# A ring of six places, four front transfers onto all partitions, and gathers that run upwards

## The chip, the cores and the metric

The kernel runs on one NeuronCore of a Trainium2 chip. Its engines are TensorE (PE), VectorE (DVE), ScalarE (ACT), GpSimd (POOL) and SyncE (SP); each runs its own instruction stream, and they meet through semaphores. Transfers between memory and the on-chip SBUF are carried by 16 DMA engines, which the queues of SP, ACT and POOL share. The metric is the device time of one execution in microseconds (us); the number that counts is the median over several runs.

## The reference

Eight batches of 8192 rows of 512 numbers are masked by a length, summed cumulatively along the rows, and the sum at half the length is taken; that one row per batch is multiplied by a 512x512 matrix.

```python
B, S, D = 8, 8192, 512                       # x: B x S x D float32
pos = np.arange(S)[None, :, None]
mask = (pos < lengths[:, None, None]).astype(np.float32)
cs = np.cumsum(x * mask, axis=1)
midpoints = (lengths // 2).clip(0)
mid_features = cs[np.arange(B), midpoints, :]
return np.matmul(mid_features[:, None, :], w).squeeze(1)
```

So output row b is the sum of the rows 0 to length//2 of batch b (as far as the mask lets them count), times `w`. Lengths are drawn between 16 and 8191; in the draw that is timed, half a length goes up to 3858 rows. No cumulative sum is needed, only a sum of the first rows of each batch, and which rows those are is known only on the chip.

## The kernel before

The sum is made by TensorE: a matmul whose weights are 0 or 1 adds rows of `x` into one PSUM row per batch (`s_ps`). Four consecutive rows form a group of 8 KB, which lies on one partition, so a chunk is 128 groups (1 MB) and takes four products, one for each row u of the group (`add`, L295). The four products go to four column groups of the array and are summed at the end.

**The front.** The first 256 rows of every batch are loaded blind, before the lengths are known. SP issues eight transfers (L117-L122), one per batch, of 64 groups each: even batches onto partitions 0 to 63 of `xf`, odd ones onto 64 to 127. Batch 7 leaves out its first 128 rows here; they come late, as `xb`, one row per partition (L195). Pairs of batches then form four chunks, for which VectorE makes the weights `wf`.

**The rest.** Rows from 256 on are gathered. VectorE works out from the lengths how many groups each batch needs, numbers them through in one list over all batches, and writes for every chunk c the row numbers `idx[:, c]`; entries past the end get a number out of bounds, and nothing is moved for them. It does this for all 61 chunks that the longest lengths could need (`ge`, `z`, `idx`), then makes weights for all 61 (`early`, `wc`). Each VectorE step waits for the one before it (`step`, L206-L210), and every one of them shows up in the profile with line L210.

GpSimd issues one indirect transfer per chunk (L173) into a ring of eight places `xt`, the chunk c into place c % 8. It and TensorE go downwards, from the count of needed chunks to chunk 0, and each chunk has code of its own. To get into it, both jump through a tree of compares (`enter`, L139-L155) past the chunks that this draw does not need: 25 of 61 are used. Chunk 0 is the one with padding and has a place of its own, `xz`, which ScalarE fills with zeros before. A place is free when TensorE has counted it into `s_free` (L327); GpSimd waits for that at L188. Behind the last gather, on the same queue, GpSimd issues `xb` and two transfers for `w` (L195-L198).

**The end.** When the last chunk and `xb` are in, VectorE copies `s_ps` to SBUF in four quarters, TensorE folds the four column groups and turns the result over (L336, four matmuls into four PSUM tiles), VectorE copies these four, TensorE multiplies by `w` (L344), VectorE copies the result, and SP and ACT each store half of it (L135).

Of the kernel before, what the change touches and what calls it, by code (L numbers as in the profile page):

```python
# [11 lines left out]
P = 128  # L12
# [3 lines left out]
def kernel(  # L16
# [13 lines left out]

# [6 lines left out]
    R = 8  # L37
    UB = S // U
    HEAD = 256
    HU = HEAD // U  # L40
    PAIRS = B // 2
    C = -(-B * (S // 2 // U + 1 - HU) // P)
# [12 lines left out]
    def sem(name):  # L55
        return tc.alloc_semaphore(name)

    xf = sb("xf", [P, PAIRS, U * D])
    xb = sb("xb", [P, D])
    xt = sb("xt", [P, R, U * D])  # L60
    xz = sb("xz", [P, U * D])
# [4 lines left out]
    k_f = sb("k_f", [1, B])  # L66
    qe = sb("qe", [1, B])
    up_i = sb("up_i", [1, 1], I32)
    count = sb("count", [1, 1], I32)
    pad = sb("pad", [1, 1])  # L70
    row = sb("row", [1, 4 * B])
# [4 lines left out]
    base = sb("base", [P, 1], I32)  # L76
    rank4 = sb("rank4", [P, 1])
    rank = sb("rank", [P, 1])
    q_i = sb("q_i", [P, C], I32)
    v_i = sb("v_i", [P, C * U], I32)  # L80
    f_i = sb("f_i", [P, U], I32)
    f_m = sb("f_m", [P, U], I32)
    q = sb("q", [P, C])
    v4 = sb("v4", [P, C * U])
    z = sb("z", [P, C, B + 1])
    ge = sb("ge", [P, C, B])
    idx = sb("idx", [P, C], I32)
    early = sb("early", [P, C, U, B])
    wc = sb("wc", [P, C, U, B])
    wf = sb("wf", [P, PAIRS * (U * B + 2)])  # L90
# [9 lines left out]
    mf_ps = [ps(f"mf_ps{k}", [P, D]) for k in range(KC)]  # L100
    o_ps = ps("o_ps", [P, D])
    bc_ps = ps("bc_ps", [P, D])

    s_full = [sem(f"full{c}") for c in range(C)]
    s_front = [sem(f"front{k}") for k in range(PAIRS)]
    s_back = sem("back")
    s_w = [sem(f"w{k}") for k in range(2)]
    s_len, s_out, s_pool, s_dve, s_pe, s_free, s_zero = (
        sem(n) for n in ("len", "out", "pool", "dve", "pe", "free", "zero"))

    END = "gather_end"
    LAST = slice(D - P, D)
    QUARTERS = [slice(k, D - P, KC - 1) for k in range(KC - 1)] + [LAST]


    def sync(sp):
        for b in range(B):  # L117
            skip = P if b == B - 1 else 0
            at = 64 * (b % 2)
            sp.dma_start(out=xf[at + skip // U:at + HU, b // 2],  # L120
                         in_=x[b, skip:HEAD].rearrange("(q u) d -> q (u d)", u=U),
                         ).then_inc(s_front[b // 2], 16)  # L122
        store(sp, 0)
        sp.wait_ge(s_out, 32)


    def scalar(act):
        act.dma_start(out=lens[:], in_=lens_words).then_inc(s_len, 16)
        act.memzero(xz[:])  # L129
        act.memzero(xf[64:64 + P // U, PAIRS - 1]).then_inc(s_zero, 1)  # L130
        store(act, 2)
# [6 lines left out]

    def enter(eng, name, count):  # L139

        def node(lo, hi, label):
            with nc.body(label, valid_engines=[eng.engine]):
                mid = (lo + hi) // 2
                eng.br_cmp(count, mid, target(mid + 1, hi), target(lo, mid), "IS_GT")
            for a, e in ((mid + 1, hi), (lo, mid)):
                if a < e:
                    node(a, e, target(a, e))

        def target(lo, hi):
            if lo == hi:  # L150
                return f"{name}_c{lo - 1}" if lo else f"{name}_tail"
            return f"{name}_n{lo}_{hi}"

        eng.br(target(0, C))
        node(0, C, target(0, C))  # L155


    def gpsimd(pool):
# [7 lines left out]
        pool.iota(f_i[:], pattern=[[1, U]], base=0, channel_multiplier=U)  # L166
        pool.iota(fold_i[:], pattern=[[-1, B]], base=128, channel_multiplier=1)
        pool.iota(v_i[:], pattern=[[P * U, C], [1, U]], base=HEAD, channel_multiplier=0,  # L168
                  ).then_inc(s_pool, 1)
        pool.sem_inc(s_free, R)  # L170

        def gather(to, c):
            pool.indirect_dma_start(  # L173
                out=to, out_offset=None, in_=xu,
                in_offset=bass.IndirectOffsetOnAxis(ap=idx[:, c:c + 1], axis=0),
                bounds_check=B * UB - 1, oob_is_err=False,
            ).then_inc(s_full[c], 16)
# [4 lines left out]
        pool.wait_ge(s_zero, 1)  # L182
        enter(pool, "gp", n)
        for c in range(C - 1, -1, -1):
            with nc.body(f"gp_c{c}", valid_engines=[pool.engine]):
                pool.wait_ge(s_dve, marks["idx"])
                if c:
                    pool.sem_inc(s_free, -1)._wait_ge(s_free, 1)  # L188
                    gather(xt[:, c % R], c)
                    pool.br(f"gp_c{c - 1}")  # L190
                else:
                    gather(xz[:], c)
                    pool.br("gp_tail")
        with nc.body("gp_tail", valid_engines=[pool.engine]):
            pool.dma_start(out=xb[:], in_=x[B - 1, :P]).then_inc(s_back, 16)  # L195
            pool.dma_start(out=wt[:, :KC - 1],
                           in_=w[:D - P].rearrange("(p k) d -> p k d", k=KC - 1)).then_inc(s_w[0], 16)
            pool.dma_start(out=wt[:, KC - 1], in_=w[LAST]).then_inc(s_w[1], 16)  # L198
            pool.drain()
            pool.br(END)  # L200

# [4 lines left out]
    def vector(dve):  # L206
# [6 lines left out]
        def mark(name):  # L213
# [8 lines left out]
        mark("ones")  # L222
        dve.wait_ge(s_pool, 5)
        step(ts, out=p4[:], in0=p_i[:], scalar1=2, scalar2=None, op0=ALU.logical_shift_right)
        step(stt, out=rank[:], in0=p4[:], scalar=-63.0, in1=base[:], op0=ALU.mult, op1=ALU.add)
        step(ts, out=q[:], in0=q_i[:], scalar1=rank[:], scalar2=None, op0=ALU.add)
        step(ts, out=z[:, :, B], in0=q[:], scalar1=float(FAR), scalar2=None, op0=ALU.add)
        dve.wait_ge(s_len, 16)
        step(ts, out=l8[:], in0=lens[:, ::2], scalar1=3, scalar2=None, op0=ALU.logical_shift_right)
        step(ts, out=k_f[:], in0=l8[:], scalar1=float(1 - HU), scalar2=0.0, op0=ALU.add, op1=ALU.max)  # L230
        step(dve.tensor_tensor_scan, out=qe[:], data0=k_f[:], data1=zero[:, :B], initial=0.0,
             op0=ALU.add, op1=ALU.add)
        step(ts, out=up_i[:], in0=qe[:, B - 1:], scalar1=float(P - 1), scalar2=None, op0=ALU.add)
        step(ts, out=count[:], in0=up_i[:], scalar1=7, scalar2=None, op0=ALU.logical_shift_right)
        mark("count")
        step(stt, out=pad[:], in0=count[:], scalar=float(P), in1=qe[:, B - 1:], op0=ALU.mult,
             op1=ALU.subtract)
        step(stt, out=row[:, :B], in0=qe[:], scalar=pad[:], in1=k_f[:], op0=ALU.add,
             op1=ALU.subtract)
        step(ts, out=row[:, B:B + 1], in0=pad[:], scalar1=-1.0, scalar2=float(HU - FAR),  # L240
             op0=ALU.mult, op1=ALU.add)
        step(ts, out=row[:, B + 1:2 * B], in0=k_f[:, :B - 1], scalar1=-1.0, scalar2=float(UB),
             op0=ALU.mult, op1=ALU.add)
        step(ts, out=l2[:], in0=lens[:, ::2], scalar1=1, scalar2=None, op0=ALU.logical_shift_right)
        step(stt, out=row[:, 2 * B:3 * B], in0=l2[:], scalar=1.0, in1=lens[:, ::2], op0=ALU.add,
             op1=ALU.min)
        step(stt, out=row[:, 3 * B:], in0=row[:, :B], scalar=float(U), in1=row[:, 2 * B:3 * B],
             op0=ALU.mult, op1=ALU.add)
        mark("row")
        dve.wait_ge(s_pe, 1)  # L250
        starts, jumps, rows, ends = (bc_ps[:, k * B:(k + 1) * B] for k in range(4))
        step(tt, out=ge[:], in0=q[:].unsqueeze(2).to_broadcast((P, C, B)),
             in1=starts.unsqueeze(1).to_broadcast((P, C, B)), op=ALU.is_ge)
        step(tt, out=z[:, :, :B], in0=ge[:], in1=jumps.unsqueeze(1).to_broadcast((P, C, B)),
             op=ALU.mult)
        step(dve.tensor_reduce, out=idx[:], in_=z[:], axis=AX.X, op=ALU.add)
        mark("idx")
        step(dve.memset, wf[:], 0.0)
        step(dve.memset, wb[:], 0.0)
        dve.wait_ge(s_pool, 6)  # L260
        step(ts, out=f_m[:], in0=f_i[:], scalar1=HEAD - 1, scalar2=None, op0=ALU.bitwise_and)
        diag = wf[:].rearrange("p (f e) -> p f e", f=PAIRS)
        for h in range(2):
            at = slice(64 * h, 64 * h + 64)
            step(tt, out=diag[at, :, h:h + U * B:B],
                 in0=f_m[at].unsqueeze(1).to_broadcast((64, PAIRS, U)),
                 in1=rows[at, h::2].unsqueeze(2).to_broadcast((64, PAIRS, U)), op=ALU.is_lt)
# [3 lines left out]
        step(tt, out=early[:].rearrange("p c u b -> p (c u) b"),  # L271
             in0=v4[:].unsqueeze(2).to_broadcast((P, C * U, B)),
             in1=ends.unsqueeze(1).to_broadcast((P, C * U, B)), op=ALU.is_lt)
        step(tt, out=wc[:], in0=early[:], in1=ge[:].unsqueeze(2).to_broadcast((P, C, U, B)),
             op=ALU.mult)
        step(ts, out=fold_m[:], in0=fold_i[:], scalar1=31, scalar2=None, op0=ALU.bitwise_and)
        step(tt, out=wb[:, B - 1:], in0=p_i[:], in1=rows[:, B - 1:], op=ALU.is_lt)
        step(dve.memset, fold[:], 0.0)
        step(ts, out=fold[:, :, 0], in0=fold_m[:], scalar1=0, scalar2=None, op0=ALU.is_equal)
        mark("w")  # L280
        dve.wait_ge(s_pe, 2)
# [7 lines left out]
        dve.wait_ge(s_pe, 3 + KC)  # L289
        step(dve.tensor_copy, out=o_sb[:], in_=o_ps[:, :P])  # L290
        mark("out")


    def tensor(pe):
        def add(j, weights, rows, cols=slice(0, D)):  # L295
# [95 lines left out]
```

## Time and profile before

| | us |
|---|---|
| three runs | 95.44, 94.98, 94.63 |
| median | 94.98 |
| the profiled execution | 95.83 |
| its span in the profile | 93.7 |
| PE busy | 48.6 |
| POOL busy | 28.7 |
| DVE busy | 14.2 |
| ACT busy | 5.1 |

The span runs from the first to the last instruction of the program in the profile; the execution's own time is 2.1 us longer. The page cuts the span into 40 slices and gives for each how busy the engines were, the share of the DMA engines' time that was used, and the rate in GB/s. Queue q1 in its third part carries the transfers that SP issues, q0 those of GpSimd; instructions are fetched through q8 and q14. Matmuls of 32-bit numbers appear as two each, and a chunk as eight.

### The profile page before, as it was taken

How to read it: one execution, taken by the hardware profiler on the slowest of the kernel's cores; microseconds unless marked ns; L12 is line 12 of the kernel's file. 1: busy time of each engine (PE TensorE's matmuls, PEld its weight loads, DVE VectorE, ACT ScalarE, POOL GpSimd, SP SyncE). 2: the span in 40 equal slices, each digit the busy share in tenths (PEclk: the TensorE clock that was granted, in tenths of full speed). 3: DMA queues.
4: the chain of work that ended last, by engine and by line, in shares of the span. 5: the costliest groups of instructions: out<-in, count | busy, mean ns of one | idle time of the engine just before them, and what ended most of it. 6: DMA issues, size and time to landing. Idle time of an engine off the chain costs nothing. (4 is left out here: it accounts for less than half of the span.)

```text
span 93.7 us, 856 instructions
## 1 busy us (share of the span) xinstructions
PE 48.6 (52%) x298; PEld 7.4 (8%) x298; DVE 14.2 (15%) x43; ACT 5.1 (5%) x3; POOL 28.7 (31%) x41
## 2 busy tenths in 40 slices
PE   1820834265200029995444477533677887479820
PEld 0120000000000002210000000000000000001700
DVE  3868995000000000000000000000000000000710
ACT  3980000000000000000000000000000000000000
POOL 5300002778710000677748423553830000000000
PEclk9999999999999999999999555999555555966998
DMA  0999999999999999999999999999999999995000
GB/s 0 238 224 224 220 224 213 224 224 399 413 420 430 406 423 413 420 416 430 413 427 416 430 427 413 430 402 427 416 430 416 427 413 430 408 410 227 9 10 4
DMA packets 4557, 31.26 MB, mean 334 GB/s; under 512 B 621, under 2 KB 653, under 8 KB 909
## 3 DMA queue, kind: packets, MB, share of 16 engines
q0 software_dynamic: 3904, 27.21, 70.5%
q1 hardware_dynamic: 626, 3.94, 19.2%
q8 instruction: 5, 0.08, 0.4%
q14 instruction: 2, 0.02, 0.1%
q10 hardware_dynamic: 20, 0.01, 0.0%
HBM read 31.46 MB, written 0.02 MB: 336 GB/s over the span
## 5 line engine op out<-in xcount | busy, mean ns | idle before, releaser
L296 PE MATMUL s_ps<-xt,wc 128*8 128x512 f32 x192 | 33.5, 805 | 27.1 <-DMA xt<-in_x_dram,idx 16.5
L173 POOL DMA_INDIRECT xt<-in_x_dram,idx x24 | 24.0, 1001 | 38.6 <-POOLq L188 34.4
L296 PE MATMUL s_ps<-xf,wf 128*8 128x512 f32 x32 | 7.6, 1040 | 9.9 <-DMA xf<-in_x_dram 6.6
L210 DVE COPY s_sb<-s_ps 128x128 f32<-128x128 f32 x4 | 1.2, 292 | 71.2 <-PE s_ps L296 71.1
L296 PEld LDWEIGHTS s_ps<-xt,wc 128*8 128x8 f32 x192 | 3.7, 93 | 56.9 <-DMA xt<-in_x_dram,idx 39.1
L304 PE MATMUL s_ps<-zero 1*32 1x512 f32 x8 | 1.9, 1055 | 1.9 <-DVE ones L210 1.9
L210 DVE TENSOR_TENSOR wc<-early,ge 128x1952 f32<-128x1952 f32 x1 | 2.2, 2193 | 0.0
L210 DVE TENSOR_TENSOR early<-v,bc_ps 128x1952 f32<-128x1952 f32 x1 | 2.2, 2187 | 0.0
L129 ACT ACTIVATE xz<-xz 128x2048 uint32<-128x2048 uint32 x1 | 1.9, 1909 | 0.0
L130 ACT ACTIVATE xf<-xf 32x2048 uint32<-32x2048 uint32 x1 | 1.9, 1905 | 0.0
L296 PE MATMUL s_ps<-xz,wc 128*8 128x512 f32 x8 | 1.8, 980 | 0.0
L296 PEld LDWEIGHTS s_ps<-xf,wf 128*8 128x8 f32 x32 | 0.5, 90 | 15.4 <-DMA xf<-in_x_dram 11.9
L336 PE MATMUL mf_ps<-fold,s_sb 128*128 128x32 f32 x8 | 1.4, 286 | 0.4 <-DVE s_sb L210 0.4
L307 PE MATMUL bc_ps<-row,ones 1*128 1x32 f32 x2 | 0.6, 408 | 1.6 <-DVE row L210 1.6
L129 ACT ACT_TABLE_LOAD x1 | 1.3, 1283 | 1.5 <-SPq L47 1.5
L344 PE MATMUL o_ps<-wt,mf_sb 128*32 128x128 f32 x32 | 1.3, 285 | 0.0
L336 PEld LDWEIGHTS mf_ps<-fold,s_sb 128*128 128x128 f32 x8 | 1.2, 188 | 0.8 <-DVE s_sb L210 0.7
L173 POOL DMA_INDIRECT xz<-in_x_dram,idx x1 | 1.0, 993 | 0.3 <-issue 0.3
L168 POOL IOTA v_i<- 128x244 int32 x1 | 0.9, 857 | 0.0
L210 DVE COPY mf_sb<-mf_ps 128x32 f32<-128x32 f32 x4 | 0.8, 192 | 0.4
L210 DVE TENSOR_TENSOR ge<-q,bc_ps 128x488 f32<-128x488 f32 x1 | 0.7, 664 | 0.7 <-PE bc_ps L307 0.7
L160 POOL IOTA base<- 32x1 int32 x4 | 0.5, 124 | 0.8 <-SPq L47 0.6
(49 smaller groups left out, 13.2 us busy)
## 6 DMA issues: line engine op xcount, KB each, us to landing
xf<-in_x_dram SPq DMA_DIRECT2D x7, 512.0 KB, 9.3
wt<-in_w_dram POOLq DMA_DIRECT2D x1, 768.0 KB, 19.4
xt<-in_x_dram,idx POOLq DMA_INDIRECT x24, 15.6
xf<-in_x_dram SPq DMA_DIRECT2D x1, 256.0 KB
xb<-in_x_dram POOLq DMA_DIRECT2D x1, 256.0 KB, 18.1
wt<-in_w_dram POOLq DMA_DIRECT2D x1, 256.0 KB, 19.5
lens<-in_lengths_dram ACTq DMA_DIRECT2D x1, 0.1 KB
xz<-in_x_dram,idx POOLq DMA_INDIRECT x1, 18.4
```

Of the source, the lines that this page charges most:

```text
L129: act.memzero(xz[:])
L130: act.memzero(xf[64:64 + P // U, PAIRS - 1]).then_inc(s_zero, 1)
L160: pool.iota(base[32 * k:32 * k + 32], pattern=[[0, 1]], base=64 * (k % 2) + 8 * (k // 2) + 63 * 8 * k, channel_multiplier=16).then_inc(s_p ...
L168: pool.iota(v_i[:], pattern=[[P * U, C], [1, U]], base=HEAD, channel_multiplier=0,).then_inc(s_pool, 1)
L173: pool.indirect_dma_start(out=to, out_offset=None, in_=xu, in_offset=bass.IndirectOffsetOnAxis(ap=idx[:, c:c + 1], axis=0), bounds_check=B ...
L210: do(*args, **kw).then_inc(s_dve, 1)
L296: return pe.matmul(s_ps[32 * j:32 * j + B, cols], lhsT=weights, rhs=rows, start=False, stop=False, skip_group_check=True, tile_position=(0 ...
L304: pe.matmul(to[32 * j:32 * j + 32, :width], lhsT=zero[:, :32], rhs=zero[:, :width], start=True, stop=False, skip_group_check=True, tile_po ...
L307: pe.matmul(bc_ps[:, :4 * B], lhsT=ones[:], rhs=row[:], start=True, stop=True,).then_inc(s_pe, 1)
L336: pe.matmul(mf_ps[k][:, :4 * B], lhsT=s_sb[:, k * P:(k + 1) * P], rhs=fold[:].rearrange("p b r -> p (b r)"), start=True, stop=True).then_i ...
L344: mm = pe.matmul(o_ps[32 * j:32 * j + 32, :P], lhsT=mf_sb[:, k], rhs=wt[:, k, j * P:(j + 1) * P], start=False, stop=(k == KC - 1), skip_gr ...
```

## The change

**The front** is four transfers instead of eight, each of two batches: group q of batch 2f goes to partition 2q of chunk f, that of batch 2f+1 to partition 2q+1. Batch 7's first 256 rows are in it too; its next 128 rows are what comes late as `xb` (`BACK`), and its gathers begin at row 384 (`R0`).

**One ring.** `xt` has six places and holds the front as well: blind chunks in places 0 to 3, gathered chunk c in place (c + 4) % 6. ScalarE clears places 4 and 5 at the start, `xf` and `xz` are gone. A gather waits for TensorE's count of finished chunks, `s_done`.

**TensorE loops.** The blind chunks have their own code; after them six bodies, one for each place, are run round and round, with a compare against the number of chunks, a step down of `s_wr` and a wait for `s_full[s]` against a register. Since a body's weights must lie at a fixed address, they lie in `wr`, six places too; ScalarE copies the weights of each chunk from `wc` into its place, in a loop of its own that waits for `s_done` against a register.

**GpSimd runs upwards**: gather 0 stands in its first block of code, chunks 1, 2, 3 and so on follow behind the tail's code, each with a compare that leaves for the tail (a jump back) once the count is reached. The tail loads `w` in three parts instead of two.

**VectorE** makes the row numbers in two parts, 8 chunks first (gather 0 waits for those alone), then 53; the weights as well. What TensorE broadcasts comes in two rows, `row` and `row2`. Eleven small fills come first. The weights of the blind chunks for even and odd partitions are made by two steps over all partitions.

**Fewer copies**: `s_ps` is copied in two halves instead of four quarters, the folded result as one copy instead of four, and the eight matmuls that clear PSUM become two.

```diff
-    R = 8
+    R = 6
 def sync(sp):
-        for b in range(B):
-            skip = P if b == B - 1 else 0
-            at = 64 * (b % 2)
-            sp.dma_start(out=xf[at + skip // U:at + HU, b // 2],
-                         in_=x[b, skip:HEAD].rearrange("(q u) d -> q (u d)", u=U),
-                         ).then_inc(s_front[b // 2], 16)
+        for f in range(PAIRS):
+            sp.dma_start(out=xt[:, f],
+                         in_=x[2 * f:2 * f + 2, :HEAD].rearrange("b (q u) d -> q b (u d)", u=U),
+                         ).then_inc(s_front[f], 16)
...
 def scalar(act):
-        act.memzero(xz[:])
-        act.memzero(xf[64:64 + P // U, PAIRS - 1]).then_inc(s_zero, 1)
-        store(act, 2)
+        for s in range(PAIRS, R):
+            act.memzero(xt[:, s]).then_inc(s_zero, 1)
+        act.wait_ge(s_dve, marks["w0"])
+        for s in range(PAIRS, R):
+            act.copy(out=weights_of(s), in_=wc[:, s - PAIRS]).then_inc(s_wr, 1)
...
+        for s in range(R):
+            with nc.body(f"ac_0_{s}", valid_engines=[act.engine]):
+                act.br_cmp(left, R + s, f"ac_1_{s}", "ac_end", "IS_GT")
+            with nc.body(f"ac_1_{s}", valid_engines=[act.engine]):
+                act.wait_ge(s_done, free)
+                col = act.snap(free)
+                act.copy(out=weights_of(s),
+                         in_=wc[:, bass.ds(col + (R - PAIRS - 1), 1)].rearrange("p c e -> p (c e)"),
+                         ).then_inc(s_wr, 1)
+                act.reg_add(free, free, 1)
+                if s == R - 1:
+                    act.reg_sub(left, left, R)
+                act.br(f"ac_0_{(s + 1) % R}")
...
 def gpsimd(pool):
+        def gather(c):
+            s = (c + PAIRS) % R
+            if c < R - PAIRS:
+                pool.wait_ge(s_zero, c + 1)
+            else:
+                pool.wait_ge(s_done, c + PAIRS - R + 1)
             pool.indirect_dma_start(
-                out=to, out_offset=None, in_=xu,
+                out=xt[:, s], out_offset=None, in_=xu,
...
-        enter(pool, "gp", n)
-        for c in range(C - 1, -1, -1):
-            with nc.body(f"gp_c{c}", valid_engines=[pool.engine]):
-                pool.wait_ge(s_dve, marks["idx"])
...
+        pool.wait_ge(s_dve, marks["idx0"])
+        gather(0)
+        pool.wait_ge(s_dve, marks["count"])
+        pool.load(n, count[:])
+        pool.wait_ge(s_dve, marks["idx"])
+        pool.br("gp_1")
         with nc.body("gp_tail", valid_engines=[pool.engine]):
...
+        for c in range(1, C):
+            with nc.body(f"gp_{c}", valid_engines=[pool.engine]):
+                pool.br_cmp(n, c, f"gp_go{c}", "gp_tail", "IS_GT")
+            with nc.body(f"gp_go{c}", valid_engines=[pool.engine]):
+                gather(c)
+                pool.br(f"gp_{c + 1}" if c + 1 < C else "gp_tail")
...
 def vector(dve):
+        table(0, C1)
+        mark("idx0")
...
+        table(C1, C)
         mark("idx")
...
-        for k in range(KC):
-            step(dve.tensor_copy, out=s_sb[:, k * P:(k + 1) * P], in_=s_ps[:, QUARTERS[k]])
+        for at in HALVES:
+            step(dve.tensor_copy, out=s_sb[:, at], in_=s_ps[:, at])
         mark("s")
-        for k in range(KC):
-            dve.wait_ge(s_pe, 3 + k)
-            step(dve.tensor_copy, out=mf_sb[:, k], in_=mf_ps[k][:, :4 * B])
+        dve.wait_ge(s_pe, 4)
+        step(dve.tensor_copy, out=mf_sb[:], in_=mf_ps[:])
...
 def tensor(pe):
+        def chunk(s):
+            for u in range(U):
+                mm = add(u, weights_of(s)[:, u * B:(u + 1) * B], xt[:, s, u * D:(u + 1) * D])
+            mm.then_inc(s_done, 1)
+
         pe.wait_ge(s_dve, marks["front"])
         for f in range(PAIRS):
...
+            pe.wait_ge(s_front[f], 16)
+            chunk(f)
+        pe.br(f"pe_0_{PAIRS}")
+        for s in range(R):
+            with nc.body(f"pe_0_{s}", valid_engines=[pe.engine]):
+                pe.br_cmp(left, s, f"pe_1_{s}", "pe_end", "IS_GT")
+            with nc.body(f"pe_1_{s}", valid_engines=[pe.engine]):
+                pe.sem_inc(s_wr, -1)._wait_ge(s_wr, 1)
+                pe.wait_ge(s_full[s], full)
+                chunk(s)
+                if s == R - 1:
+                    pe.reg_sub(left, left, R)
+                if s == PAIRS - 1:
+                    pe.reg_add(full, full, 16)
+                pe.br(f"pe_0_{(s + 1) % R}")
```

More of the change, by code (lines that the diff above doesn't have):

```diff
@@ L65 @@
     l2 = sb("l2", [1, B], I32)
-    k_f = sb("k_f", [1, B])
-    qe = sb("qe", [1, B])
+    kk = sb("kk", [1, B])
+    negk = sb("negk", [1, B])
+    jump = sb("jump", [1, B - 1])
+    r0 = sb("r0", [1, B])
+    mm_ = sb("mm_", [1, B])
+    row = sb("row", [1, 2 * (B + 1)])
+    row2 = sb("row2", [1, 2 * B])
+    nr = sb("nr", [1, B])
     up_i = sb("up_i", [1, 1], I32)
     count = sb("count", [1, 1], I32)
-    pad = sb("pad", [1, 1])
-    row = sb("row", [1, 4 * B])
+    chunks = sb("chunks", [1, 1], I32)
     ones = sb("ones", [1, P])
@@ L99 @@
     s_ps = ps("s_ps", [P, D])
-    mf_ps = [ps(f"mf_ps{k}", [P, D]) for k in range(KC)]
+    mf_ps = ps("mf_ps", [P, KC, 4 * B])
     o_ps = ps("o_ps", [P, D])
     bc_ps = ps("bc_ps", [P, D])
-    s_full = [sem(f"full{c}") for c in range(C)]
+    b2_ps = ps("b2_ps", [P, D])
+    s_full = [sem(f"full{k}") for k in range(R)]
     s_front = [sem(f"front{k}") for k in range(PAIRS)]
[L106 to L109, printed above, removed]
+    s_w = [sem(f"w{k}") for k in range(3)]
@@ L111 @@
+    s_len, s_back, s_out, s_pool, s_dve, s_pe, s_done, s_wr, s_zero = (
+        sem(n) for n in ("len", "back", "out", "pool", "dve", "pe", "done", "wr", "zero"))
     END = "gather_end"
[L112 to L122 removed]
+    HALVES = [slice(0, D // 2), slice(D // 2, D)]
@@ L222, in vector @@
         mark("ones")
+        K = [1 - r // U for r in R0]
+        for t, values in ((negk, [-k for k in K]), (kk, K), (r0, R0)):
+            for at in (slice(0, B - 1), slice(B - 1, B)):
+                step(dve.memset, t[:, at], float(values[at][0]))
+        step(dve.memset, jump[:, :B - 2], float(UB - K[0]))
+        step(dve.memset, jump[:, B - 2:], float(UB - K[B - 2] + (R0[B - 1] - R0[B - 2]) // U))
+        step(dve.memset, row[:, :1], 0.0)
+        step(dve.memset, row[:, B + 1:B + 2], float(R0[0] // U))
+        step(dve.memset, row[:, 2 * B + 1:], float(FAR))
         dve.wait_ge(s_pool, 5)
@@ L231, in vector @@
-        step(dve.tensor_tensor_scan, out=qe[:], data0=k_f[:], data1=zero[:, :B], initial=0.0,
+        step(tt, out=mm_[:], in0=l8[:], in1=negk[:], op=ALU.max)
+        step(dve.tensor_tensor_scan, out=row[:, 1:B + 1], data0=kk[:], data1=mm_[:], initial=0.0,
              op0=ALU.add, op1=ALU.add)
-        step(ts, out=up_i[:], in0=qe[:, B - 1:], scalar1=float(P - 1), scalar2=None, op0=ALU.add)
+        step(tt, out=row[:, B + 2:2 * B + 1], in0=jump[:], in1=mm_[:, :B - 1], op=ALU.subtract)
+        mark("row")
@@ L234, in vector @@
+        step(ts, out=up_i[:], in0=row[:, B:B + 1], scalar1=1.0, scalar2=float(P - 1), op0=ALU.max,
+             op1=ALU.add)
         step(ts, out=count[:], in0=up_i[:], scalar1=7, scalar2=None, op0=ALU.logical_shift_right)
         mark("count")
[L236 to L241, printed above, removed]
@@ L249, in vector @@
[L249 to L256, printed above, removed]
-        mark("idx")
@@ new lines, in vector @@
+        mark("chunks")
+        table(C1, C)
+        mark("idx")
+        step(dve.memset, wr[:], 0.0)
+        step(ts, out=half[:], in0=p_i[:], scalar1=1, scalar2=None, op0=ALU.logical_shift_right)
+        step(ts, out=odd[:], in0=p_i[:], scalar1=1, scalar2=None, op0=ALU.bitwise_and)
+        for h in range(2):
+            step(ts, out=out_of[:], in0=odd[:], scalar1=float(FAR * (1 - 2 * h)),
+                 scalar2=float(FAR * h), op0=ALU.mult, op1=ALU.add)
+            step(stt, out=first[:, h:h + 1], in0=half[:], scalar=float(U), in1=out_of[:],
+                 op0=ALU.mult, op1=ALU.add)
@@ L298, in add @@
                              tile_position=(0, 32 * j))
-        n = pe.alloc_register("n_pe")
+        left = pe.alloc_register("left_pe")
+        full = pe.alloc_register("full_pe")
         pe.wait_ge(s_dve, marks["ones"])
         for to, width in ((s_ps, D), (o_ps, P)):
-            for j in range(4):
-                pe.matmul(to[32 * j:32 * j + 32, :width], lhsT=zero[:, :32], rhs=zero[:, :width],
-                          start=True, stop=False, skip_group_check=True, tile_position=(0, 32 * j))
@@ L306, in tensor @@
-        pe.wait_ge(s_dve, marks["row"])
-        pe.matmul(bc_ps[:, :4 * B], lhsT=ones[:], rhs=row[:], start=True, stop=True,
-                  ).then_inc(s_pe, 1)
-        pe.load(n, count[:])
+            pe.matmul(to[:, :width], lhsT=zero[:, :P], rhs=zero[:, :width], start=True, stop=False,
+                      skip_group_check=True)
+        for name, to, of in (("row", bc_ps, row), ("row2", b2_ps, row2)):
+            pe.wait_ge(s_dve, marks[name])
+            pe.matmul(to[:, :of.shape[1]], lhsT=ones[:], rhs=of[:], start=True, stop=True,
+                      ).then_inc(s_pe, 1)
@@ L330, in tensor @@
+        with nc.body("pe_end", valid_engines=[pe.engine]):
+            pe.wait_ge(s_dve, marks["back"])
             pe.wait_ge(s_back, 16)
```

192 lines of the change are left out of this document (93 added, 99 removed).

## The prediction

> **What bounds the kernel now.** I read the page first (span, slices, queues), then busy time in stretches chosen from it, then the chain that ended last, then the timeline.
>
> ```profile
> span 93.7 us, 856 instructions
> ...
> GB/s 0 238 224 224 220 224 213 224 224 399 413 420 430 406 423 413 420 416 430 413 427 416 430 427 413 430 402 427 416 430 416 427 413 430 408 410 227 9 10 4
> ...
> q0 software_dynamic: 3904, 27.21, 70.5%
> q1 hardware_dynamic: 626, 3.94, 19.2%
> ```
> ```profile
> 2.30:21.00 18.70, 8.27 (x42) 1.24 (x34) 11.16 (x32) 4.27 (x3) 4.98 (x5) 1.00 1.01 223
> 21.00:84.00 63.00, 34.91 (x200) 3.79 (x200) 0.00 (x0) 0.00 (x0) 22.51 (x24) 0.83 1.01 419
> 21.00:34.40 13.40, 1.90 (x8) 0.12 (x8) 0.00 (x0) 0.00 (x0) 3.97 (x4) 1.00 1.00 413
> ```
>
> In the second view the last three numbers are granted clock, DMA share and GB/s. The DMA share is 1.0 from 2.3 to 84 us, so transfers bound the kernel; PE is busy 35 us of the 63 of the long stretch. But the rate has two levels: 223 GB/s while SP's front (q1, `xf`) moves, 419 once the gathers (q0) do. Section 3 says the same per packet: 19.2% of 16 engines x 93.7 us over 3.94 MB is 0.60 us per 8 KB; 70.5% over 27.21 MB is 0.32 us. A front row costs twice a gathered row. So the front takes 3.94 MB / 0.223 = 17.7 us, from 2.3 to 20.0.
>
> ```profile
> 82.57 0.04 issue
> 82.61 3.93 PE s_ps L296 x24
> ...
> 86.56 0.30 DVE s_sb L210
> ...
> 86.91 1.38 PE mf_ps L336 x8
> 88.29 1.24 PE o_ps L344 x32
> ...
> 89.56 0.29 DVE o_sb L210
> ```
>
> The chain ends with the last full gather landing at 82.6, 3.93 us of PE for it, for the part chunk and for `xb`, then 3.3 us of copies and small matmuls. Anything that brings the landing forward brings the end forward.
>
> **The front.** Eight transfers onto partitions 0-63 or 64-127 become four onto all 128, even partitions one batch, odd the other; batch 7's first 128 rows, formerly loaded late, come with it, so it is 4 x 1.05 = 4.19 MB. The trace has no SP transfer onto 128 partitions, so its rate is bounded by the nearest rows: 223 (SP, half the partitions) and 419 (POOL, all of them). Which of the two differences matters, queue or partitions? This look at half a microsecond holds packets of q1 alone:
>
> ```profile
> q1 hardware_dynamic: 20, 0.16, 94.3%
> ...
> xf<-in_x_dram SPq DMA_DIRECT2D x1, 512.0 KB, 10.2
> ```
>
> It is the stretch from 2.9 to 3.4 us: 94.3% of 16 x 0.5 us over 20 packets is 0.38 us each, when the transfers had just begun. The hardware queue can therefore move 8 KB well below 0.60 us, so I put the loss on the destinations. I take 413, the rate of the gathers' first stretch (less than 419, as the order of rows in memory is new): 4.19 / 0.413 = 10.2 us. The front ends at 12.5 instead of 20.0: **-7.5 us**. At 419 it is -7.7; at 223 it is 18.8 us, +1.1.
>
> [...]
>
> **Bytes of the gathers.** Batch 7 starts its gathers 32 groups later, so by the lengths of this draw 3161 gathered rows of 8 KB become 3129: 24 full chunks of 128 and a part, as before. Before the last full landing lie 24 full chunks in both. Nothing.
>
> **Can the gathers follow at 12.5?** These rows are the start and one chunk pitch near the end:
>
> ```profile
> 0.93 0.51 ACTq L128 DMA_DIRECT2D lens<-in_lengths_dram  x1
> 1.69 0.17 DVE L210 MEMSET ones<- 1x128 f32 x1
> 2.53 0.60 DVE L210 TENSOR_SCALAR q<-q_i,rank 128x61 f32<-128x61 int32 x1
> 3.17 0.22 DVE L210 TENSOR_SCALAR z<-q 128x61 f32<-128x61 f32 x1
> 3.49 0.16 DVE L210 TENSOR_SCALAR l<-lens 1x8 int32<-1x8 int32 x1
> 3.69 0.16 DVE L210 TENSOR_SCALAR k_f<-l 1x8 f32<-1x8 int32 x1
> 5.61 0.15 DVE L210 SCALAR_TENSOR_TENSOR row<-row 1x8 f32<-1x8 f32 x1
> 6.49 0.66 DVE L210 TENSOR_TENSOR ge<-q,bc_ps 128x488 f32<-128x488 f32 x1 [0.72 <-PE bc_ps L307]
> 7.88 0.73 DVE L210 TENSOR_REDUCE idx<-z 128x61 int32<-128x549 f32 x1
> 9.77 1.89 PE L296 MATMUL s_ps<-xf,wf 128*8 128x512 f32 x8 [3.32 <-DVE wf L210]
> 12.54 2.19 DVE L210 TENSOR_TENSOR wc<-early,ge 128x1952 f32<-128x1952 f32 x1
> 15.21 0.09 DVE L210 MEMSET fold<- 128x32 f32 x1
> 15.32 0.18 DVE L210 TENSOR_SCALAR fold<-fold_m 128x8 f32<-128x8 int32 x1
> 15.71 1.19 POOL L173 DMA_INDIRECT xt<-in_x_dram,idx  x1 [12.62 <-POOLq L188]
> 34.46 8.04 PE L296 MATMUL s_ps<-xt,wc 128*8 128x512 f32 x56 [10.52 <-issue]
> 80.12 1.04 PE L296 MATMUL s_ps<-xt,wc 128*8 128x512 f32 x8 [0.70 <-DMA xt<-in_x_dram,idx]
> 82.61 1.90 PE L296 MATMUL s_ps<-xt,wc 128*8 128x512 f32 x8 [1.44 <-DMA xt<-in_x_dram,idx]
> ```
>
> A small VectorE step costs 0.20 us (3.49 to 3.69), a small fill 0.11 (15.21 to 15.32). After: fills of `zero` and `ones` to 1.9, eleven more fills 1.2, `p4`, `rank` and the 61-column step 1.0, four small steps 0.8: `row` at 4.9 (now 5.8). Then 0.7 of broadcast and three steps on 8 of 61 columns at 0.27 each (488 elements 0.66, a small one 0.16): `idx0` near 6.5, now 8.6 for the whole. Five small steps 1.0, the other 53 columns 2.1, the fill of `wr` and six small steps 1.4, two of the diagonal 0.4: `front` at 11.4, now 9.7; 1.7 later, hidden as long as the transfers have work queued.
>
> Now `idx` is there at 8.6, yet the first gather starts at 15.71, after a jump across the unused chunks' code; PE starts gathered chunks at 34.46, after 10.52 us idle with no releaser. Both engines jump 36 chunks ahead; the two stretches hold instruction packets:
>
> ```profile
> q14 instruction: 1, 0.01, 0.9%
> ...
> q8 instruction: 2, 0.03, 1.2%
> ```
>
> The first is of 12 to 16 us, the second of 24 to 34.5. I read both waits as code fetched through busy DMA engines. Neither cost anything: the front covered the one, eight free places of `xt` the other. In the changed kernel gather 0 is straight code behind `idx0` and the rest runs on upwards, so gathers 0 and 1, into the two cleared places, are issued by about 8 and 11: ahead of 12.5. They last 2 x 2.49 us (80.12 to 82.61), to 17.5. Gather 2 needs place 0, thus PE's first blind chunk: 11.4 + 1.9 = 13.3, plus 1.0 us of issue, 14.3. `lens` shows at most 2.6 us from issue to use (0.93 to 3.49), so its data flow by 16.9: 0.6 us to spare. Later ones need one PE chunk each, at most 1.9 us, against 2.49 of transfer. So: nothing, with a thin cover that is the third rival.
>
> **The ring.** PE adds a compare, a branch, a semaphore step and a register wait per chunk; ScalarE a copy of 128x32.
>
> ```profile
> L129 ACT ACTIVATE xz<-xz 128x2048 uint32<-128x2048 uint32 x1 | 1.9, 1909 | 0.0
> L210 DVE COPY s_sb<-s_ps 128x128 f32<-128x128 f32 x4 | 1.2, 292 | 71.2 <-PE s_ps L296 71.1
> L210 DVE COPY mf_sb<-mf_ps 128x32 f32<-128x32 f32 x4 | 0.8, 192 | 0.4
> ```
>
> The copy lies between 0 and 1.9 us (64 times the elements); by VectorE's 128x32 copy I take 0.2. It starts when the place's old chunk is done, five chunks (12 us) before PE needs it; behind it on ScalarE waits only the next copy. PE's idle 0.6 to 1.4 us per chunk hides up to 0.6 of loop steps while its chunks take 1.9. At the end, where nothing hides them, I put 0.1 for three passes (0 to 0.5). POOL's backward jump to its tail comes after the last gather's issue, with some five chunks queued; even 7 us of code fetch (8.6 to 15.71) fits in those 12.
>
> **The end.** Copies of 128x256 cost 0.29 + 128 x 1.04 ns (292 less 192 over 96 elements) = 0.43; two end at 0.9. The last two quarters' matmuls 0.7 (half of 1.38), one copy 0.33 with its gap, 32 matmuls 1.24, copy 0.33: 3.5 against 3.3. Overlap lost exceeds copies saved: **+0.2** (-0.1 to +0.4).
>
> **Sum:** -7.5 + 0.1 + 0.2 = -7.2. Span 93.7 becomes 86.5. The profiled execution took 95.83, 2.1 us around its span and 0.85 above the median 94.98 of the runs; the shift goes on the median: **87.8**. Its own range: a warm PE on the last two chunks saves up to 0.86 each (1.90 to 1.04), 86.0 with a front at 419; a front a tenth slower (370) costs 1.1 more, 89.2 with 0.3 more for the loop at the end.
>
> **Rivals.**
> *The front stays slow* (0.13), ending on the other side. If the limit is SP's queue, or the even/odd order makes engines meet on the same destinations, 4.19 MB at 223 takes 1.1 us more than now: 94.98 + 1.1 + 0.3 = 96.4. It decides at 237 GB/s: 4.19 / 0.237 = 17.7. For it: every long q1 stretch runs at 223; against it: the 0.38 us packets.
> *A slower front still* (0.03). Two batches 16 MB apart (8192 x 512 x 4 B) are read in turn; if they met on the same memory, at half of 223, the front would take 37.4 us: 87.8 + 27 = 115. The rows speak against it: chunks that cross batches run at the same 2.49 pitch. [...]
> *The transfers run dry between front and ring* (0.13). VectorE's 61 columns took 0.60 beside POOL's iota, 0.22 alone: the two delay each other. If gathers 0 and 1 (1 us each) hold `front` back, or VectorE holds the gathers back, gather 2 comes 2 to 3 us late: 90.5. At worst the first gather waits for all of VectorE's work, as 15.71 right after 15.50 could also mean, and most of the gain goes; PE's like wait with VectorE idle speaks against it.
> *PE fetches its loop again at each wrap* (0.04). 10.5 us of wait and about 8 for six chunks (two at 1.9, four at 1.04) make 18.5 a turn against 14.9 of transfers; four turns cost 14: 102. Up to about 6.7 us per wrap it is free; it ends slower from 8.7.
>
> **Numbers.** The forecast has 0.67. With the dry ring that is 0.80, and both are faster by over 1%, about what a measurement here can tell from no change. The slow front gives 95.5 to 97: 0.05 of its 0.13 within 1%, 0.08 slower; the other two, 0.07, slower. Range 86.0 to 92.5, the forecast's and the dry ring's together.
>
> **What would show it.** q1 near 420 GB/s and the slice rate flat from 3 us; the front landed by 13, first gather before 10; PE's 10.5 us wait gone; chunk pitch 2.49 still; last full landing near 75. Wrong: 223 GB/s before 20 us, a gap in DMA between 13 and 20, or a PE wait at each sixth chunk.

## The result and the profile after

| | before | changed |
|---|---|---|
| median of 4 runs, us | 95.21 | 86.40 |
| range, us | 94.63 to 95.76 | 85.85 to 86.85 |
| ratio to the kernel before | 1 | 0.907 (0.899 to 0.915) |
| span of the profiled execution, us | 93.7 | 84.7 |

The change makes the kernel 9% faster; 87.8 was forecast, with 86.0 to 92.5 as the range. All ratios here leave out runs in which the whole core was disturbed, so that one experiment below, the front in halves, has a median well above what its ratio says and a profile of such a run (100.83 us).

The page of the changed kernel, its rate in 40 slices and its queues:

```profile
GB/s 0 275 418 422 430 430 426 422 402 383 414 426 426 418 433 433 414 426 422 418 422 426 418 430 414 422 430 414 426 430 414 418 422 418 408 395 188 0 2 5
...
q0 software_dynamic: 3984, 26.95, 77.0%
q1 hardware_dynamic: 594, 4.20, 12.3%
```

The two levels are gone: from the third slice on the rate is that of the gathers, but for 402 and 383 in two slices just behind the hand-over. SP's queue q1 now takes 12.3% of 16 x 84.7 us for 512 packets of 8 KB, 0.33 us each, where it took 0.60.

The same by stretches (last three numbers: granted clock, DMA share, GB/s):

```profile
2.30:12.50 10.20, 4.37 (x16) 2.03 (x19) 8.03 (x41) 4.19 (x3) 3.07 (x4) 1.00 1.00 402
12.50:75.00 62.50, 40.94 (x220) 3.61 (x212) 5.03 (x8) 5.34 (x25) 25.77 (x27) 0.72 1.01 419
```

The start and the end of the timeline (start, duration, engine, line):

```profile
5.97 0.24 DVE L230 TENSOR_REDUCE idx<-z 128x8 int32<-128x80 f32 x1
...
7.16 1.19 POOL L194 DMA_INDIRECT xt<-in_x_dram,idx  x1 [4.00 <-DVE chunks L230]
...
10.34 1.02 POOL L194 DMA_INDIRECT xt<-in_x_dram,idx  x1 [1.98 <-DVE first L230]
...
11.45 6.51 PE L346 MATMUL s_ps<-xt,wr 128*8 128x512 f32 x40 [3.83 <-DVE wr L230]
...
14.16 0.99 POOL L194 DMA_INDIRECT xt<-in_x_dram,idx  x1 [2.81 <-PE s_ps L346]
...
14.87 1.93 DVE L230 TENSOR_TENSOR wc<-early,ge 128x1696 f32<-128x1696 f32 x1
...
15.87 1.79 POOL L194 DMA_INDIRECT xt<-in_x_dram,idx  x1 [0.72 <-issue]
...
18.67 1.04 PE L346 MATMUL s_ps<-xt,wr 128*8 128x512 f32 x8 [0.71 <-DMA xt<-in_x_dram,idx]
...
21.82 1.36 PE L346 MATMUL s_ps<-xt,wr 128*8 128x512 f32 x8 [2.10 <-DMA xt<-in_x_dram,idx]
...
71.67 1.89 PE L346 MATMUL s_ps<-xt,wr 128*8 128x512 f32 x8 [0.60 <-DMA xt<-in_x_dram,idx]
```

Both waits that the prediction read as fetches of code are gone: GpSimd's first gather starts 0.95 us after its row numbers, and PE runs from its first blind chunk into the gathered ones without a pause.

And the chain that ended last, its last steps:

```profile
74.14 3.58 PE s_ps L346 x24
77.75 0.44 DVE s_sb L230
78.23 1.12 PE mf_ps L395 x8
79.37 0.30 DVE mf_sb L230
79.72 1.12 PE o_ps L403 x32
80.87 0.29 DVE o_sb L230
```

The last full gather is taken up at 74.14 instead of 82.61. The account of the span: 8.5 us from that landing, 0.35 from the last sums (3.58 for 3.93), 0.1 lost in the copies (3.41 for 3.29), 0.3 gained after the last copy (3.85 before, 3.54 now; why, was not looked for): 9.0 together.

### The profile page after: what moved, and what is told of

Same layout as the page of the kernel before. It is cut to its first block, busy times and chain, and to the rows that moved or that the text cites. A ratio compares the mean times of both kernels' runs of the same rounds, so it can differ in the third digit from the quotient of the medians.

```text
span 84.7 us, 1017 instructions
## 1 busy us (share of the span) xinstructions
PE 50.6 (60%) x288; PEld 8.4 (10%) x288; DVE 15.4 (18%) x57; ACT 10.3 (12%) x28; POOL 30.0 (35%) x43
## 3 DMA queue, kind: packets, MB, share of 16 engines
q1 hardware_dynamic: 594, 4.20, 12.3%
## 4 chain that ended last, share of the span: by engine, by line
DMA 55%; PE 21%; DVE 11%; issue 7%; POOLq 0%; DVEq 0%; POOL 0%; SPq 0%
DMA xt<-in_x_dram,idx 55%; PE s_ps L346 17%; DVE z L230 1%; PE o_ps L403 1%; PE mf_ps L395 1%; DVE idx L230 1%; DVE ge L230 1%; DVE row L230 1%; DVE wr L230 1%; PE bc_ps L358 1%; DVE zero L230 1%; DVE s_sb L230 1%; DVE first L230 0%; DVE l L230 0%; DVE out_of L230 0%
## 5 line engine op out<-in xcount | busy, mean ns | idle before, releaser
L346 PE MATMUL s_ps<-xt,wr 128*8 128x512 f32 x232 | 44.4, 870 | 25.4 <-DMA xt<-in_x_dram,idx 21.6
L194 POOL DMA_INDIRECT xt<-in_x_dram,idx x25 | 25.8, 1030 | 35.5 <-PE s_ps L346 27.6
L156 ACT COPY wr<-wc 128x32 f32 x23 | 5.0, 218 | 45.0 <-PE s_ps L346 39.5
L346 PEld LDWEIGHTS s_ps<-xt,wr 128*8 128x8 f32 x232 | 4.1, 93 | 64.3 <-DMA xt<-in_x_dram,idx 56.0
L140 ACT ACTIVATE xt<-xt 128x2048 uint32<-128x2048 uint32 x2 | 3.7, 1901 | 0.0
L354 PE MATMUL s_ps<-zero 1*128 1x512 f32 x2 | 2.1, 1136 | 1.9 <-DVE ones L230 1.9
L230 DVE TENSOR_TENSOR wc<-early,ge 128x256 f32<-128x256 f32 (+1 forms) x2 | 2.4, 1176 | 0.1
L230 DVE TENSOR_TENSOR early<-v,b_ps 128x256 f32<-128x256 f32 (+1 forms) x2 | 2.3, 1171 | 0.1
L212 POOL DMA_DIRECT2D wt<-in_w_dram x2 | 1.1, 580 | 0.0
L230 DVE TENSOR_REDUCE idx<-z 128x8 int32<-128x80 f32 (+1 forms) x2 | 0.9, 471 | 0.1
```

What stands on the lines that cost most here:

```text
L140: act.memzero(xt[:, s]).then_inc(s_zero, 1)
L156: act.copy(out=weights_of(s), in_=wc[:, bass.ds(col + (R - PAIRS - 1), 1)].rearrange("p c e -> p (c e)"),).then_inc(s_wr, 1)
L194: pool.indirect_dma_start(out=xt[:, s], out_offset=None, in_=xu, in_offset=bass.IndirectOffsetOnAxis(ap=idx[:, c:c + 1], axis=0), bounds_c ...
L212: pool.dma_start(out=wt[:, k], in_=w[QUARTERS[k]]).then_inc(s_w[k - 1], 16)
L230: do(*args, **kw).then_inc(s_dve, 1)
L346: return pe.matmul(s_ps[32 * j:32 * j + B, cols], lhsT=weights, rhs=rows, start=False, stop=False, skip_group_check=True, tile_position=(0 ...
```

## The experiments

**The new front alone.** In the kernel before, only the front is changed; for the byte count to stay, the late transfer of 128 rows and its four products fall away.

```diff
-        for b in range(B): ...           # eight transfers, 64 partitions each
+        for f in range(PAIRS):
+            sp.dma_start(out=xf[:, f],
+                         in_=x[2 * f:2 * f + 2, :HEAD].rearrange("b (q u) d -> q b (u d)", u=U),
+                         ).then_inc(s_front[f], 16)
...                                       # weights by even and odd partition, as in the change
-            pool.dma_start(out=xb[:], in_=x[B - 1, :P]).then_inc(s_back, 16)
```

> The kernel before with the new front alone: four transfers onto all partitions, even and odd, batch 7's first 128 rows among them, so that the late transfer of 128 rows and its four products fall away; the bytes in all stay as before. Theory (front and early gathers both count): q1 at about 415 GB/s, front landed by 13 us, but the first gather still starts near 15 us after its wait for code, so the transfers lie idle from about 12.7 to 17; gathers start 3 us sooner than before, 92 us. Rival (the front is all of it): 87 us, no gap.

Measured: 90.5 us (89.26 to 90.96) against 95.7 of the kernel before on the same chip; no interval was formed. Four stretches of its profile, and the rows of its first gather and its first gathered chunk:

```profile
12.60:20.00 7.40, 4.19 (x28) 0.62 (x20) 3.81 (x6) 0.00 (x0) 6.18 (x5) 0.93 0.94 324
20.00:33.00 13.00, 3.75 (x20) 0.74 (x24) 0.00 (x0) 0.00 (x0) 3.43 (x4) 0.51 1.01 422
33.00:40.00 7.00, 5.54 (x56) 1.15 (x48) 0.00 (x0) 0.00 (x0) 4.99 (x6) 1.00 0.93 328
40.00:78.00 38.00, 22.75 (x120) 1.68 (x112) 0.00 (x0) 0.00 (x0) 12.04 (x13) 0.69 1.01 422
```
```profile
10.88 1.19 POOL L173 DMA_INDIRECT xt<-in_x_dram,idx  x1 [7.80 <-DVE wf L209]
...
29.25 8.72 PE L301 MATMUL s_ps<-xt,wc 128*8 128x512 f32 x64 [12.47 <-issue]
```

By the spans, 88.3 us for 93.7, the front gives 5.4 of the 9.0 us by itself. Most of the rest is lost in two dips: 7.4 us at 324 instead of 422 after the front, 1.7 us, and 7.0 us at 328, 1.6 us. The second follows PE's wait of 12.47 us into its chunk code: eight gathers fill the eight places, and GpSimd waits 9.0 us until PE frees one. What makes the first dip is not shown. Its DMA share is 0.94, so for the most part packets took longer and the queues were not empty; the third gather, issued at 13.69, took 2.95 us beside a VectorE step. In the kernel before the same wait cost nothing (413 GB/s from 21.0 to 34.4 us). The gap I expected was longer, since the first gather came at 10.88, not 15.

**The front in halves.** The changed kernel, with eight transfers of 64 partitions.

```diff
-            sp.dma_start(out=xt[:, f], in_=x[2 * f:2 * f + 2, :HEAD]...
+            at = 64 * (b % 2)
+            sp.dma_start(out=xt[at:at + 64, b // 2], in_=x[b, :HEAD]...
```

> The changed kernel with its front put back to eight transfers of 64 partitions each, the same bytes. Theory (destinations): q1 falls to 223 GB/s, the front takes 18.8 instead of 10.2 us, 95 us. Rival (ring, loops, early gather 0 bring the gain): 86 to 88 us.

Measured: ratio 1.008 (0.999 to 1.017), so the whole gain is gone, with the ring, the loops and the early gather in place. Its first stretch of front:

```profile
5.00:28.00 23.00, 6.50 (x28) 1.26 (x28) 11.20 (x32) 2.49 (x6) 5.97 (x5) 1.00 1.01 217
```

The hardware queue is the same as in the changed kernel, the rate about half, 217 GB/s for 402. With the stripes below, which have the same eight transfers of 64 rows, this leaves the destinations.

**The front in stripes.** Eight transfers of 64 groups, each onto every second partition.

```diff
+            sp.dma_start(out=xt[b % 2::2, b // 2], in_=x[b, :HEAD]...
```

> The changed kernel with its front as eight transfers of 64 groups, each onto every second partition of all 128, so that the data end where they do in the changed kernel. Theory (which partitions a transfer spans): q1 near 415 GB/s, 86.5 us. Rival 1 (a transfer has to have 128 rows): 223 GB/s, 95 us. Rival 2 (the DMA engines step through their rows in time and meet on half of the destinations): between, 90 us or more.

Measured: ratio 0.910 (0.901 to 0.919), the changed kernel's within the interval. Two stretches:

```profile
2.30:8.00 5.70, 3.32 (x8) 1.76 (x7) 4.20 (x27) 4.19 (x3) 1.70 (x3) 1.00 0.98 328
8.00:14.50 6.50, 3.05 (x16) 0.60 (x20) 5.80 (x16) 0.34 (x2) 1.71 (x3) 1.00 1.00 420
```

So 64 rows a transfer are no hindrance if they spread over all partitions. The first 6 us are slower, which the second rival would have for the whole front; why it rights itself was not tried.

**The front in blocks.** Four transfers of 128 partitions, batch after batch instead of alternating.

```diff
-                         in_=x[2 * f:2 * f + 2, :HEAD].rearrange("b (q u) d -> q b (u d)", u=U),
+                         in_=x[2 * f:2 * f + 2, :HEAD].rearrange("b (q u) d -> b q (u d)", u=U),
```

> The changed kernel with its four transfers ordered batch by batch: batch 2f on partitions 0 to 63, batch 2f+1 on 64 to 127, in one transfer of 128 partitions. Theory (only the span of partitions counts): 86.4 us. [...]

Measured: 168.5 us, ratio 1.760 (1.747 to 1.774). Its slices, 4.2 us each:

```profile
GB/s 12 51 214 299 59 51 55 51 132 179 51 55 53 53 210 96 55 53 53 79 232 51 51 55 16 126 434 415 434 415 432 411 434 415 425 421 413 405 35 4
```

Where only the front moves the rate is 51 to 55 GB/s, an eighth of 422, and most of the 16 engines' time goes unused: from 24 to 36 us the DMA share is 0.22, at 63 GB/s. The span of partitions is the same as in the changed kernel, where the front ran at 402 GB/s, so my theory that only this counts fell: the order "even, odd" counts as well. What in the order does it is not shown. By 101.4 us 9.4 MB have moved (99.1 us at 95 GB/s), the 4.19 of the front and five gathers (the humps at 132 to 299); from 108 us to 158 the slices read 405 to 434.

**Gather 0 late.** It waits for all weights.

```diff
-        pool.wait_ge(s_dve, marks["idx0"])
+        pool.wait_ge(s_dve, marks["w"])
         gather(0)
```

> The changed kernel with gather 0 held back until VectorE has made all weights (16.8 us instead of 7.2). Theory (the gathers must be in the queue when the front ends at 12.7): idle transfers from 12.7 to about 18.3, 86.4 + 5.6 = 92 us. Rival (the early gather 0 is worth nothing, the ring's start sets the time): 87 us or less.

Measured: ratio 0.989 (0.982 to 0.996), 94.5 us. Its stretches:

```profile
13.20:19.60 6.40, 3.66 (x28) 0.57 (x20) 4.20 (x7) 0.91 (x5) 1.57 (x2) 1.00 0.01 1
19.60:28.00 8.40, 2.90 (x16) 0.24 (x16) 0.00 (x0) 0.22 (x1) 5.60 (x6) 0.64 0.97 366
```

Nothing moves for 6.4 us, and the next 8.4 run at 366 (1.1 us more). So here the front's gain is there only if the gathers are queued by the time it ends. Why the rate then comes up slowly is open.

**Eight places and five places.**

```diff
-    R = 6
+    R = 8        # and in the other kernel: R = 5
```

> The changed kernel with eight places instead of six, so that gathers 0 to 3 wait for no blind chunk. The changed kernel's chunks 1 and 2 lie 3.14 us apart instead of 2.49, at 18.67 and 21.81. Theory (gather 2 came 0.6 us late): the pitch there becomes 2.5, the last full gather lands 0.6 us sooner, 85.8 us. Rival (that gap is the transfers' own): 86.4 us.

Measured: ratio 0.897 (0.890 to 0.904), not to be told from the changed kernel's 0.907. From 12 to 25 us its rate and, in the second fence, that of the changed kernel:

```profile
12.00:25.00 13.00, 8.63 (x64) 1.32 (x56) 5.52 (x10) 2.10 (x11) 9.42 (x9) 1.00 1.01 422
```
```profile
12.00:25.00 13.00, 9.07 (x60) 1.37 (x56) 5.49 (x9) 1.86 (x9) 7.73 (x7) 0.90 1.01 415
```

422 against 415 over 13 us is 0.2 us. The long pitch between 18.67 and 21.82 was not 0.6 us of idle transfers, and the last full gather is not earlier, as its chain shows: the theory was wrong, six places lose next to nothing.

```profile
74.44 2.28 PE s_ps L346 x24
```

> The changed kernel with five places. Gather 1 then waits for PE's first blind chunk at 13.4 us and is the one that comes late: gather 0's transfers last from 12.7 to 15.2, gather 1's data flow from about 16.6, 1.5 us of gap beside the 0.6 that is there: 87.5 to 88 us. Rival (six places are no thinner than five, PE's pace sets the steady part): 86.4, or, if five places starve the transfers all along, over 90 us with a pitch above 2.49.

Measured: ratio 0.921 (0.914 to 0.929), 88.2 us. Its hole:

```profile
14.80:17.20 2.40, 2.40 (x16) 0.46 (x12) 2.20 (x4) 0.00 (x0) 1.75 (x2) 1.00 0.63 140
17.20:75.00 57.80, 35.92 (x192) 2.85 (x184) 0.53 (x3) 5.23 (x24) 24.39 (x27) 0.71 1.01 420
```

2.4 us at 140 are 1.6 us lost, as expected, and after it the steady rate is full: the ring's size matters at the hand-over alone. The intervals of five and six places just touch (0.914 and 0.915), so it is the hole in the trace that shows the loss. Of five, six and eight, six is the smallest that covers it.

**The old end.**

```diff
-        for at in HALVES:
-            step(dve.tensor_copy, out=s_sb[:, at], in_=s_ps[:, at])
+        for k in range(KC):
+            step(dve.tensor_copy, out=s_sb[:, k * P:(k + 1) * P], in_=s_ps[:, QUARTERS[k]])
...                                       # and four copies of the folded result
```

> The changed kernel with the old end: four quarter copies of the sums, four copies of the folded result. From the end of the last sum to the end of the last copy the changed kernel takes 3.44 us, the kernel before 3.29. Theory (overlap lost exceeds copies saved): 3.3 us, 86.25. Rival (fewer copies are a gain that something else hid): 3.6 us or more.

Measured: ratio 0.899 (0.891 to 0.908), not told apart by time. Its chain at the end:

```profile
74.08 2.66 PE s_ps L347 x24
76.76 0.30 DVE s_sb L230
77.11 1.38 PE mf_ps L395 x8
78.49 1.24 PE o_ps L402 x32
79.75 0.29 DVE o_sb L230
```

From 76.76 to 80.04 are 3.28 us, where the changed kernel takes 3.41 (77.75 to 81.16). Fewer copies cost 0.13, by one profile of each.

**Keeping PE fast.** The last 24 sums took 3.58, 2.66 and 2.28 us in the changed kernel, with the old end and with eight places, which do the same there. In the changed kernel PE's granted clock was 0.60 over them; a gathered chunk took 1.04 us at 1.00 (61.56) and 1.89 at 0.50 (71.67). Two products with zero weights are added to each gathered chunk, first with one partition read.

```diff
+                for j in range(2):
+                    pe.matmul(s_ps[32 * j:32 * j + B, :], lhsT=zero[:, :B], rhs=zero[:],
+                              start=False, stop=False, skip_group_check=True,
+                              tile_position=(0, 32 * j))
                 pe.sem_inc(s_wr, -1)._wait_ge(s_wr, 1)
```

> The changed kernel with two products of zeros added to the sums ahead of each gathered chunk's waits, on PE alone, so that it stays busier. In the changed kernel the last 24 sums took 3.58 us, with eight places 2.28, with the old copies 2.66: the clock that PE happens to have there. Theory (the end waits for a slow PE): the last sums take 2.3 to 2.8 us including the added ones, 85.5 us. Rival (the added work delays each chunk, or the clock does not follow): 86.4 to 87.5.

> The changed kernel with the zeros, the old end of eight copies and eight places together. Theory: 0.9 us of PE clock, 0.13 of the end, and some 0.2 of the places: 85.2 us. Rival (each is within what the clock gives or takes by itself): 86.4.

Measured: ratios 1.180 (1.170 to 1.189), and with the old end and eight places 1.162 (1.153 to 1.170). A late stretch of the first:

```profile
55.00:90.00 35.00, 35.00 (x120) 2.19 (x120) 0.00 (x0) 1.52 (x7) 9.67 (x12) 0.50 0.82 276
```

PE is busy without a break, its granted clock is 0.50 (it was 1.00 until about 27 us), a chunk with its zeros takes 3.6 us, and PE bounds the kernel. Then the second of these two, with the old end and eight places, reads 128 partitions; its added products also multiply their zero weights with other numbers than zeros, the weights of gathered chunks.

```diff
-                    pe.matmul(s_ps[32 * j:32 * j + B, :], lhsT=zero[:, :B], rhs=zero[:],
+                    pe.matmul(s_ps[32 * j:32 * j + B, :], lhsT=zw[:],          # 128 x 8 zeros
+                              rhs=wc[:, :D // (U * B)].rearrange("p c e -> p (c e)"),
```

> As the run before last (old end, eight places, two added products with zero weights per gathered chunk), but the added products read all 128 partitions instead of one. With one partition PE was busy nine tenths of the span and its granted clock stayed at 0.5 throughout. Theory (what the clock follows is how much of the array works, not the time it is busy): with 128 partitions the clock comes up, a chunk with its added products takes 2.1 us, below the 2.49 of its transfer, the pitch stays 2.49, and the last sums are fast: 85 us. Rival (added products of zeros, or the two column groups alone, keep the clock down): the pitch is 3.6 us again, 110 us.

Measured: ratio 0.902 (0.899 to 0.906), 86.2 us. The steady part, and the same of the changed kernel:

```profile
25.00:74.00 49.00, 36.93 (x236) 6.00 (x230) 0.00 (x0) 3.05 (x14) 16.42 (x19) 1.00 1.01 420
```
```profile
25.00:74.00 49.00, 31.52 (x160) 2.27 (x152) 0.00 (x0) 3.48 (x16) 18.04 (x20) 0.67 1.01 422
```

The clock is full, 1.00 for 0.67, and the kernel no faster: transfers bound the steady part, and at the end the added products stand in the way of the last chunk, whose sums are done 3.0 us after its landing:

```profile
74.42 1.04 PE s_ps L349 x8
...
77.47 0.30 DVE s_sb L231
```

No kernel here is shown to beat the changed one.

**GpSimd's code from the last chunk to the first.**

```diff
-        for c in range(1, C):
+        for c in range(C - 1, 0, -1):
```

> The changed kernel with GpSimd's chunk code laid out from the last chunk to the first, so that it jumps over 60 unused chunks to chunk 1 and then runs backwards. Theory (a wait for code counts only where nothing is queued): the second gather comes at 12.5 to 17 us instead of 10.3, gather 0 covers until 15.2, later waits lie behind five queued chunks; 86.4 to 88.5 us. Rival (each backward step fetches again): the pitch of the gathers rises over 2.49, 95 us or more.

Measured: ratio 0.900 (0.892 to 0.907). The built program lays blocks of code out in the order in which control flows, and every engine's instructions are the same as the changed kernel's, so this tells nothing of the direction; it is a repeat, and shows how far two measurements of one kernel lie apart (0.900 and 0.907).

## Why the prediction was right, point by point

**What bounds the kernel, and the front.** Right. Transfers bounded it, the front ran at half rate, and the half was that of the destinations: halves give the whole gain back (1.008), stripes of 64 groups keep it (0.910). My range for the front's rate was 223 to 419; it came to 402 with its start, 418 to 430 after. The slow-front rival was priced at 96.4 us; the front in halves, 1.008 of 95.2, is 96.0.

**The size of the front's term** is where the sum was short: -7.5 forecast, -8.5 measured. I ended the old front where its bytes end at 223 GB/s, 20.0 us, and let the gathers run at full rate from there. Counted in bytes at 21.0 us: the kernel before had moved 223 x 18.7 = 4.17 MB, the changed one 402 x 10.2 + 419 x 8.5 = 7.66 MB; the difference at 419 is 8.3 us. The old hand-over itself was slow (257 GB/s from 20.0 to 21.5 us, 0.6 us lost against 419), and it went with the old front. That 86.4 still lies within the range is in part luck: the range's room below the forecast was meant for PE's clock and a front at 419, and the hand-over and the 0.3 us after the last copy had no term.

**Can the gathers follow.** Right in its times: row numbers at 6.2 (6.5 forecast), gathers at 7.2, 10.3 and 14.2, blind weights at 11.4 (11.4). That it is needed is shown by gather 0 held back: 0.989 for 0.907, 7.8 us of the gain gone. The cover was as thin as forecast: at the hand-over six places lose 0.2 us, five 1.6.

**Waits for code.** That they cost nothing in the kernel before was right, and their end was put at nothing in the sum. This holds only against the old front: with the new front and the old code, dips of 1.7 and 1.6 us appear, of the 3.6 by which that span (88.3) is the longer. The second dip follows PE's wait, so PE's loop keeps some of what the front gains, though it is not seen as a gain by itself. The first is not shown to come from GpSimd's wait (its first gather starts 2.3 us after the row numbers there), and GpSimd's new code was not tried without the rest. That the waits are code being fetched rests, as in the prediction, on the instruction packets beside them, one of q14 and two of q8; no run shows more.

**The ring** cost nothing, as forecast: the pitch stays 2.49 (71.67 to 74.14 is 2.47), and PE shows no wait at its wraps. The chain counts 0.51 and 0.18 us of GpSimd's steps between a freed place and the next gather, all beside transfers. GpSimd's jump to the tail showed no wait either: its last gather ends at 64.41, the tail's first transfer is issued at 64.42. In the built program the tail stands behind the code of chunk 60, so this jump goes forwards over unused chunks, not back.

**The end.** +0.2 forecast for the copies, +0.1 measured. That the last sums' time varies with PE's clock was in my range; in the profile it gave 0.35 (3.93 us at 0.57 before, 3.58 at 0.60 now).

**The rivals.** The slower front of two batches 16 MB apart: 430 GB/s in the slices; no sign of it, and that batches so far apart would halve a rate no run shows. PE fetching its loop again: no (its 6.7 us of free wait per wrap should be 6.9, 14.9 less 8.0; nothing hangs on it). Transfers that lose time between front and ring: only with five places, a late gather 0 or the old code.

## What to carry to other kernels

Read a transfer's rate from its own stretch: a DMA share of 1.0 hid a queue at half rate here (223 GB/s), and the time per packet in the queues' part showed it (0.60 us for 8 KB, 0.33 in the changed kernel). The destinations and the order of a transfer both counted: 217 GB/s onto 64 neighbouring partitions, 51 to 55 onto all 128 batch after batch, 402 and more onto all 128 with the batches alternating. When a front gets shorter, look for what it used to cover (waits for code, the first gather, the number of free places), since here each showed once the front was short: 1.6 us behind PE's wait, 7.8 with gather 0 late, 1.6 with five places.

## What the runs showed of the hardware that was not expected

PE's granted clock does not follow its busy time alone: busy without a break it was 0.50 (35 us of 35) with products of one partition in between, and 1.00 with as many products over 128 partitions at 75% busy (36.93 of 49 us). So busy time is not enough to tell the clock; it may be how much of the array works, as that run's theory has it. The added products differ in two things, the partitions read and whether the numbers multiplied are all zeros, and no run tells these apart.

Reordering a transfer's source from "group, batch" to "batch, group", with the same bytes onto the same partitions in all, took the front from about 420 to about 53 GB/s. No run shows why.

A gather issued while VectorE multiplied two tiles (14.87 to 16.80 us) took 1.79 us on GpSimd instead of 0.99, and ended 0.86 us after that step; in the kernel with the new front alone such a gather took 2.95 us. Here only GpSimd was held up: the step took 1.93 us for 1696 columns, 1.14 ns each, and in the kernel before, with no gather beside it, 2.19 for 1952, 1.12 each. The gather at 14.16, beside the step before, took 0.99. VectorE's 61-column step on integers is the other direction: 0.60 us beside GpSimd's iota in the kernel before, 0.28 in the changed kernel without it.
